# Where the rounded half of each weight piece is made: ScalarE's cast, or a converting DMA issued by GpSimd

## The chip, the cores and the metric

The kernel runs on one NeuronCore of one Trainium2 chip. The metric is the device time of one execution in microseconds (us), taken as the median over runs. The hardware profiler gives the start and length of every instruction of one execution, the DMA packets, and the clock that was granted to TensorE.

## The reference

Two layers over 512 tokens of width 1024, all in float32. Each layer is

```
xn = rmsnorm(x);  u, q, k, v, gA, gB = split(xn @ w_in)
h  = x + (sigmoid(gA) * pool(u) * scale + sigmoid(gB) * diffattn(q, k, v)) @ w_out
hn = rmsnorm(h);  gate, up = split(hn @ w_ffn_in)
x  = h + (silu(gate) * up) @ w_ffn_out
```

`diffattn` has four heads with two softmaxes each, q and k normed and partly rotated, with a mask by chunks of 64 tokens, and a norm behind it; `pool` is a difference of window means (windows of 2, 4, 8 and 16 tokens) times a 256x256 matrix per group. The hidden width of the feed-forward part (FFN) is 2816.

## The kernel before, in words

**Two halves.** TensorE's fast float32 format (float32r) keeps only some of the bits. So every operand is split into a rounded half `hi` and a rest `lo` = value - `hi`, and every product is three matmuls into one accumulator: hi*hi, hi*lo, lo*hi (`product`, lines 210 to 218; in the profile L215, L216 and L217). `split` (L166, L167) does it: ScalarE (ACT) copies the value into a float32r tile, which rounds, and VectorE (DVE) subtracts that from the value.

**Weight pieces.** All weight matrices are cut into 244 pieces of 256 rows by 512 columns (512 KB, a tile of 128 partitions by 1024 numbers), in the order of their use (`weight_plan`). `piece` (from line 175) fetches the next one: SyncE (SP) issues a DMA from HBM into a `raw` tile (L180, three buffers), ACT casts it to `whi` (L166, eight buffers), DVE subtracts into `wlo` (L167, eight buffers). The first four pieces load into other tiles, since nothing else lies there yet.

**Blocks.** A block of four (or three, or one) pieces serves one set of products over all 512 tokens: for each of four heads the columns of q and k, of v and gate B, of u and gate A; then the output projection, and the FFN in three rounds of hidden tiles. A block's pieces are all read by its last product, so the four `whi` buffers come free one behind the other at the block's end, and the pieces for the block after next take them.

**The order.** TensorE (PE) is kept busy by a list of postponed steps: a step that needs a result of other engines is put off until PE has streamed a given number of columns (`later`, `run_due`). On each engine, the order of instructions is fixed when the program is built, by a scheduler that follows the kernel's order and its own estimates; at run time each engine takes its instructions strictly in that order, and an instruction that has to wait holds up all behind it.

**Places that the prediction speaks of.** (1) The merge of a head's two branches (`merged`): the pool product `y`, then on DVE two instructions on `ta` (L493, L494), a split of the result by ACT (L172, tile `mh`) and DVE (L173, tile `ml`), each for two halves of 128 features. The output projection reads `mh` and `ml`. (2) q and k of a token tile: ACT sums squares (L418), DVE and GpSimd (POOL) make the reciprocal root `r` (L230 on DVE, L231 on POOL, a power), DVE scales into `qn` (L422) and rotates it (L286 to L291), and PE transposes it (L221). (3) The norm in front of a layer or of the FFN (`normed`): ACT's squares (L251), `r`, DVE's `xs` (L255), PE's transposes, the split into `xh`, `xl`. POOL does nothing in the kernel before but the 80 powers and some set-up.

Of the kernel before, what the change touches and what calls it, by code (L numbers as in the profile page):

```python
# [10 lines left out]
F32 = mybir.dt.float32  # L11
# [15 lines left out]
ROT = 32  # L27
# [3 lines left out]
EPS = 1e-6  # L31
WINDOWS = (2, 4, 8, 16)
MASKED = -3.0e38
# Hidden tiles of the FFN in three rounds.
ROUNDS = ((0, 8), (8, 16), (16, 22))
# Rows of `rows`, per layer: q gain, k gain, lambda vectors, sub-norm gain.
R_QG, R_LAM, R_SG = 0, 256, 768
ORDER = (3, 2, 1, 0)
# The hidden tiles lie where the attention's tiles lay: from which tile on, under which tag, how many.
HIDDEN_AT = {0: ("qk", 4), 4: ("v", 2), 6: ("u", 2), 8: ("m", 2), 10: ("qk", 4), 14: ("v", 2), 16: ("u", 2), 18: ("m", 2),  # L40
             20: ("qk", 4)}
# How many columns TensorE streams between a step and the one of its chain that follows on TensorE.
QK_WAIT, SCORE_WAIT, PROB_WAIT, AV_WAIT, NORM_WAIT, MERGE_WAIT = 20400, 33600, 25200, 11400, 15000, 15000


def weight_plan():
    """The weight pieces in the order of their use: (name, layer, first row tile, columns)."""
    plan = []

    def block(name, layer, cols, k0=0, k1=KD):  # L50
        for k in range(k0, k1, 2):
            plan.append((name, layer, k, cols))

    def span(*parts):
        return [c for a, n in parts for c in range(a, a + n)]

    def qk(j):
        return span((1024 + 256 * j, 256), (2048 + 256 * j, 256))

    def vg(j):  # L60
        return span((3072 + 256 * j, 256), (5120 + 256 * j, 256))

    def ug(j):
        return span((256 * j, 256), (4096 + 256 * j, 256))

    for layer in range(L):
        def out(heads):
            for cb in range(2):
                for j in heads:
                    block("w_out", layer, span((512 * cb, 512)), 2 * j, 2 * j + 2)  # L70

        for i, j in enumerate(ORDER):
            block("w_in", layer, qk(j))
            if i >= 2:
                out(ORDER[i - 2:i - 1])
            block("w_in", layer, vg(j))
            if i:
                block("w_in", layer, ug(ORDER[i - 1]))
        block("w_in", layer, ug(ORDER[3]))
        out(ORDER[2:])  # L80

        def ffn_in(f):
            block("w_ffn_in", layer, span((P * f, 256), (FF + P * f, 256)))

        def ffn_out(f0, f1):
            for cb in range(2):
                block("w_ffn_out", layer, span((512 * cb, 512)), f0, f1)

        for r, (f0, f1) in enumerate(ROUNDS):
            for f in range(f0, f1, 2):  # L90
                ffn_in(f)
                if r and f == f0:
                    ffn_out(*ROUNDS[r - 1])
        ffn_out(*ROUNDS[-1])
    return plan
# [3 lines left out]
def trunk_kernel(  # L99
# [11 lines left out]
    nc = tc.nc  # L111
# [34 lines left out]
        return row.partition_broadcast(P)  # L146

    def lambdas():
        """The negated weights of the second softmax."""
        for layer in range(L):  # L150
            lam_init = 0.8 - 0.6 * math.exp(-0.3 * layer)
            lv, nl = lams[layer], neglam[layer]
            lp = sb.tile([P, 2, QK], F32, name="lp", tag="qn", bufs=3)
            nc.vector.tensor_mul(lp, lv[:, :, 0, :], lv[:, :, 1, :])
            l2 = const.tile([P, 2], F32, name=f"l2{layer}")
            nc.vector.tensor_reduce(l2, lp, axis=AX.X, op=ALU.add)
            nc.scalar.activation(l2, l2, AF.Exp)
            nc.vector.tensor_sub(nl, l2[:, 1:2], l2[:, 0:1])
            nc.vector.tensor_scalar_add(nl, nl, -lam_init)
# [2 lines left out]
    at = [0]  # L162

    def split(hi, lo, src):
        """src = hi + lo exactly, each of 12 significant bits."""
        ins = nc.scalar.copy(hi, src)  # L166
        nc.vector.tensor_sub(lo, src, hi.bitcast(F32))  # L167
        return ins

    def split_half(hi, lo, src):  # L170
        """As split, of src / 2."""
        nc.scalar.activation(hi, src, AF.Copy, scale=0.5)  # L172
        nc.vector.scalar_tensor_tensor(lo, src, 0.5, hi.bitcast(F32), op0=ALU.mult, op1=ALU.subtract)  # L173

    def piece(raw=None):
        i = at[0]
        at[0] += 1
        if raw is None:
            raw = sb.tile([P, 2, 512], F32, name="raw", tag="raw", bufs=3)
        nc.sync.dma_start(raw.rearrange("p a b -> p (a b)"), wts[i])  # L180
        hi = sb.tile([P, 2, 512], F32R, name="whi", tag="whi", bufs=8)
        lo = sb.tile([P, 2, 512], F32R, name="wlo", tag="wlo", bufs=8)
        split(hi, lo, raw)
        return [(hi[:, a, :], lo[:, a, :]) for a in range(2)]

    def wblock(n):
        """n row tiles of 512 columns: (hi, lo) by row tile."""
        return [pair for _ in range(n // 2) for pair in piece()]

    # Work that waits for other engines: (due by TensorE's columns, order, what).  # L190
    clock = [0]
    waiting = []
    count = [0]
# [4 lines left out]
        count[0] += 1  # L198

    def run_due(done=None):  # L200
        """What is due by now, or everything in its order until done()."""
        if running[0]:
            return
        running[0] = True
        while waiting and (waiting[0][0] <= clock[0] if done is None else not done()):
            heapq.heappop(waiting)[2]()
        running[0] = False
        assert done is None or done()

    def product(acc, pairs):  # L210
        """acc = the sum over pairs of (lhsT hi, lo), (rhs hi, lo)."""
        n = len(pairs)
        for i, ((ah, al), (bh, bl)) in enumerate(pairs):
            run_due()
            nc.tensor.matmul(acc, lhsT=ah, rhs=bh, start=i == 0, stop=False)  # L215
            nc.tensor.matmul(acc, lhsT=ah, rhs=bl, start=False, stop=False)  # L216
            nc.tensor.matmul(acc, lhsT=al, rhs=bh, start=False, stop=i == n - 1)  # L217
            clock[0] += 3 * acc.shape[-1]
# [3 lines left out]
        clock[0] += 2 * P  # L222

    def rsqrt_mean(ss, n, width, times=(1.0,)):
        """times * (ss / n + eps) ** -0.5, the factors each for an equal part of the columns."""
        r = sb.tile([P, width], F32, name="r", tag="r", bufs=4)
        part = width // len(times)
        for i, f in enumerate(times):
            cs = slice(i * part, (i + 1) * part)
            nc.vector.tensor_scalar(r[:, cs], ss[:, cs], 1.0 / (n * f * f), EPS / (f * f), op0=ALU.mult, op1=ALU.add)  # L230
        nc.gpsimd.tensor_tensor(r, r, mhalf[:, :width], op=ALU.pow)  # L231
        return r
# [12 lines left out]
        return [g[:, h * 512:(h + 1) * 512] for h in range(2)]  # L245

    def normed(key, t, xh, xl, g):
        """Token tile t of the residual, over its root mean square and by the gain, transposed into xh + xl."""
        xs = sb.tile([P, D], F32, name="xs", tag="mj", bufs=2)
        ss = small("ss")  # L250
        nc.scalar.activation(xs, res[t], AF.Square, accum_out=ss)  # L251
# [27 lines left out]
        return [sb.tile([P, n, S], F32R, name=name + part, tag=tag, bufs=2) for part in "hl"]  # L279

    def rotate(qn, t):
        """The first ROT of each head's features, in place."""
        ca = cos_t[:, t, :].unsqueeze(1).broadcast_to([P, 4, ROT])
        m1 = sb.tile([P, 4, ROT], F32, name="m1", tag="m1", bufs=2)
        m2 = sb.tile([P, 4, ROT], F32, name="m2", tag="m2", bufs=2)
        nc.vector.tensor_mul(m1, qn[:, :, :ROT], ca)  # L286
        for a in range(2):
            sa = sin_t[:, t, a * HALF:(a + 1) * HALF].unsqueeze(1).broadcast_to([P, 4, HALF])
            b = (1 - a) * HALF
            nc.vector.tensor_mul(m2[:, :, a * HALF:(a + 1) * HALF], qn[:, :, b:b + HALF], sa)  # L290
        nc.vector.tensor_add(qn[:, :, :ROT], m1, m2)  # L291
# [14 lines left out]
    xh, xl = new_xT()  # L306
# [20 lines left out]
    for layer in range(L):  # L327
# [9 lines left out]
            return [(h[:, c0:c1], l[:, c0:c1]) for h, l in pairs]  # L337

        def attention(j, before, then):
            """The head's inputs; its output, (1 + tanh(gate / 2)) * the normed sum, transposed, follows token by token."""  # L340
            if before is not None:
                need(*((layer, before, "s", t) for t in range(NT)))
            qh, ql = pair("q", "qk", 4)
# [105 lines left out]
            return [(hi[:, a, :], lo[:, a, :]) for a in range(2)]  # L449

        def windowed(j, c, acc, uh, ul):
            """The window means less the tile's own values, by shifted sums."""
            window = WINDOWS[j]
            up = sb.tile([P, 16 + S], F32, name="up", tag="up", bufs=2)
            nc.vector.memset(up[:, :16], 0.0)
# [12 lines left out]
            split(uh[:, c, :], ul[:, c, :], prev[:, 16:])  # L468

        def merged(j, mj, mh, ml):  # L470
            """The pool branch and the sum of both branches, transposed."""
            w = wblock(KD)
            pw = pool_weights(j)
            uh, ul = pair("u", "u", 2)
# [121 lines left out]


def constants():
    """What depends on the shapes alone: rotary factors and pool counts, by token."""
    import numpy as np  # L600

    f = np.float32
# [48 lines left out]
```

## Time and profile before

| what | value |
|---|---|
| median of three runs | 1483.15 us (1483.08 to 1483.3) |
| profiled execution, first to last instruction | 1481.0 us |
| PE busy | 1473.8 us, 6998 matmuls |
| DVE busy | 793.8 us |
| ACT busy | 531.6 us |
| POOL busy | 62.3 us |
| DMA, mean rate | 93 GB/s |
| granted TensorE clock | 1.000 |

The span of the profiled execution is 2.15 us under the median of the runs; what lies around the span (start and end of the program) makes the difference. Busy time of PE is wall time in which a matmul is under way. Matmuls overlap in PE's pipeline, so the mean length of one (0.38 to 0.40 us) is longer than the distance of two that follow each other (about 0.23 us).

### The profile page before, as it was taken

The page shows a single profiled execution, that of the slowest core. Times are in us where ns is not written, and L with a number is a line of the kernel's source. Part 1 is how long each engine was busy: PE and PEld are TensorE (multiplying, and loading weights), DVE is VectorE, ACT ScalarE, POOL GpSimd, SP SyncE. Part 2 cuts the span into 40 slices and gives each one's busy share as a digit, 9 for nine tenths or more (in the row PEclk, how much of TensorE's full clock was granted, in tenths as well). Part 3 has the DMA queues.
Part 4 walks back from the last instruction along what each step waited for, and adds up shares of the span by engine and source line. Part 5 has one row for each costly group of instructions (what it writes and reads, how often), then busy time and mean ns, then how long its engine had stood idle before and what let it go on. Part 6 is the DMA issues. An engine that isn't in the chain of part 4 may idle for free.

```text
span 1481.0 us, 18060 instructions
## 1 busy us (share of the span) xinstructions
PE 1473.8 (100%) x6998; PEld 1227.6 (83%) x6998; DVE 793.8 (54%) x1550; ACT 531.6 (36%) x1081; POOL 62.3 (4%) x87
## 2 busy tenths in 40 slices
PE   8999999999999999999999999999999999999999
PEld 6888888888988888888888888888889888888887
DVE  7767676566634334433476676766655433434331
ACT  6545343453323222312354543435433322222220
POOL 1010000000000000000010001000000000000000
PEclk9999999999999999999999999999999999999999
DMA  6322231223233223313222232222313223323311
GB/s 245 115 65 79 78 108 59 91 95 98 86 99 114 99 72 114 114 58 113 100 86 71 73 106 65 85 85 86 114 57 115 96 75 114 99 72 114 111 47 57
DMA packets 39832, 138.19 MB, mean 93 GB/s; under 512 B 4545, under 2 KB 5441, under 8 KB 39746
## 3 DMA queue, kind: packets, MB, share of 16 engines
q1 hardware_dynamic: 38450, 134.41, 27.5%
q10 hardware_dynamic: 1296, 2.62, 0.6%
q8 instruction: 55, 0.90, 0.3%
q14 instruction: 31, 0.25, 0.0%
HBM read 134.92 MB, written 2.10 MB: 93 GB/s over the span
## 4 chain that ended last, share of the span: by engine, by line
PE 98%; DVE 1%; ACT 0%; DMA 0%; POOL 0%; issue 0%; POOLq 0%; DVEq 0%; ACTq 0%
PE mm L217 30%; PE mm L215 30%; PE mm L216 30%; PE tr L221 3%; PE sc L217 1%; PE sc L216 1%; PE sc L215 1%; PE oy L217 1%; PE oy L216 1%; PE oy L215 1%; DVE xs L255 0%; DVE wlo L167 0%; ACT xs L251 0%; DMA res<-in_x 0%; DVE res L503 0%; POOL r L231 0%
## 5 line engine op out<-in xcount | busy, mean ns | idle before, releaser
L215 PE MATMUL mm<-xh,whi 128*128 128x512 f32 (+1 forms) x960 | 369.1, 385 | 0.0
L217 PE MATMUL mm<-xh,wlo 128*128 128x512 f32 (+1 forms) x960 | 367.1, 382 | 0.0
L216 PE MATMUL mm<-xl,whi 128*128 128x512 f32 (+1 forms) x960 | 366.9, 382 | 0.0
L166 ACT CAST whi<-raw 128x1024 fp32r<-128x1024 f32 x244 | 255.5, 1050 | 294.0 <-PE mm L217 139.4
L167 DVE TENSOR_TENSOR wlo<-raw,whi 128x1024 fp32r<-128x1024 f32 x244 | 297.5, 1222 | 117.2 <-ACT whi L166 109.0
L217 PEld LDWEIGHTS mm<-xh,wlo 128*128 128x128 f32 x960 | 180.4, 188 | 35.1
L216 PEld LDWEIGHTS mm<-xl,whi 128*128 128x128 f32 x960 | 180.6, 188 | 34.2
L215 PEld LDWEIGHTS mm<-xh,whi 128*128 128x128 f32 x960 | 180.5, 188 | 34.1
L215 PE MATMUL mm<-whi,xh 128*128 128x512 f32 x512 | 205.8, 402 | 0.1
L217 PE MATMUL mm<-whi,xl 128*128 128x512 f32 x512 | 200.9, 392 | 0.0
L216 PE MATMUL mm<-wlo,xh 128*128 128x512 f32 x512 | 200.7, 392 | 0.2 <-DVE wlo L167 0.2
L215 PE MATMUL mm<-whi,fh 128*128 128x512 f32 (+1 forms) x358 | 140.2, 391 | 0.0
L217 PE MATMUL mm<-whi,fl 128*128 128x512 f32 (+1 forms) x358 | 139.7, 390 | 0.0
L216 PE MATMUL mm<-wlo,fh 128*128 128x512 f32 (+1 forms) x358 | 139.1, 389 | 0.0
L503 DVE TENSOR_TENSOR res<-mm,res 128x512 f32<-128x512 f32 (+1 forms) x97 | 66.1, 683 | 132.4 <-PE mm L217 132.1
L217 PEld LDWEIGHTS mm<-whi,xl 128*128 128x128 f32 x512 | 96.3, 188 | 20.9 <-DVE xl L167 0.2
L215 PEld LDWEIGHTS mm<-whi,xh 128*128 128x128 f32 x512 | 96.5, 188 | 18.6 <-ACT xh L166 0.6
L216 PEld LDWEIGHTS mm<-wlo,xh 128*128 128x128 f32 x512 | 96.7, 189 | 18.4 <-DVE wlo L167 0.6
L231 POOL TENSOR_TENSOR r<-r,mhalf 128x1 f32<-128x1 f32 (+1 forms) x80 | 61.6, 770 | 1054.8 <-DVE r L230 979.4
L544 DVE SCALAR_TENSOR_TENSOR th<-th,mm 128x512 f32<-128x512 f32 x42 | 28.9, 688 | 122.9 <-ACT th L543 122.8
L217 PEld LDWEIGHTS mm<-whi,fl 128*128 128x128 f32 x358 | 67.4, 188 | 15.4
L216 PEld LDWEIGHTS mm<-wlo,fh 128*128 128x128 f32 x358 | 67.5, 188 | 15.0
(113 smaller groups left out, 1548.9 us busy)
## 6 DMA issues: line engine op xcount, KB each, us to landing
raw<-in_wts SPq DMA_DIRECT2D x244, 512.0 KB, 4.0
pwr<-in_pool_w ACTq DMA_DIRECT2D x8, 256.0 KB, 2.6
out<-res SPq DMA_DIRECT2D x7, 256.0 KB, 2.0
res<-in_x SPq DMA_DIRECT2D x3, 512.0 KB, 8.3
g<-in_gains SPq DMA_DIRECT2D x3, 512.0 KB, 3.7
res<-in_x ACTq DMA_DIRECT2D x1, 512.0 KB, 3.5
lv<-in_rows SPq DMA_DIRECT2D x2, 256.0 KB, 5.3
qkg<-in_rows SPq DMA_DIRECT2D x2, 128.0 KB, 6.6
```

The lines of the kernel that those rows point to most:

```text
L166: ins = nc.scalar.copy(hi, src)
L167: nc.vector.tensor_sub(lo, src, hi.bitcast(F32))
L215: nc.tensor.matmul(acc, lhsT=ah, rhs=bh, start=i == 0, stop=False)
L216: nc.tensor.matmul(acc, lhsT=ah, rhs=bl, start=False, stop=False)
L217: nc.tensor.matmul(acc, lhsT=al, rhs=bh, start=False, stop=i == n - 1)
L221: nc.tensor.transpose(dst, src, ident)
L231: nc.gpsimd.tensor_tensor(r, r, mhalf[:, :width], op=ALU.pow)
L503: nc.vector.tensor_add(res[t][:, cs], here, res[t][:, cs])
L544: nc.vector.scalar_tensor_tensor(th, th, 1.0, gate, op0=ALU.add, op1=ALU.mult)
```

## The change

From the ninth piece on, ACT's cast goes. Instead POOL issues a second DMA for the same piece, from the same place in HBM into `whi`, whose type differs from the source's, so that the DMA converts. DVE's subtraction stays; it now waits for two DMAs. The first eight pieces are split as before. What else the file differs in is comments, which moves its line numbers by four behind `piece`.

```diff
         nc.sync.dma_start(raw.rearrange("p a b -> p (a b)"), wts[i])
         hi = sb.tile([P, 2, 512], F32R, name="whi", tag="whi", bufs=8)
         lo = sb.tile([P, 2, 512], F32R, name="wlo", tag="wlo", bufs=8)
-        split(hi, lo, raw)
+        if i < 8:
+            split(hi, lo, raw)
+        else:
+            nc.gpsimd.dma_start(hi.rearrange("p a b -> p (a b)"), wts[i])
+            nc.vector.tensor_sub(lo, raw, hi.bitcast(F32))
         return [(hi[:, a, :], lo[:, a, :]) for a in range(2)]
```

The order of instructions moves with it. On DVE, the first merge of layer 0 stood like this before (`wlo` is the subtraction for the pieces of a later block, `ta` and `ml` belong to the merge):

```order
L167 TENSOR_TENSOR wlo<-raw,whi 128x1024 x3
L493 SCALAR_TENSOR_TENSOR ta<-ta,mm 128x512
L167 TENSOR_TENSOR wlo<-raw,whi 128x1024
L494 SCALAR_TENSOR_TENSOR ta<-ta,scale,mj 128x512
L493 SCALAR_TENSOR_TENSOR ta<-ta,mm 128x512
L173 SCALAR_TENSOR_TENSOR ml<-ta,mh 128x512
L494 SCALAR_TENSOR_TENSOR ta<-ta,scale,mj 128x512
L173 SCALAR_TENSOR_TENSOR ml<-ta,mh 128x512
```

and now:

```order
L187 TENSOR_TENSOR wlo<-raw,whi 128x1024 x2
L497 SCALAR_TENSOR_TENSOR ta<-ta,mm 128x512
L187 TENSOR_TENSOR wlo<-raw,whi 128x1024
L498 SCALAR_TENSOR_TENSOR ta<-ta,scale,mj 128x512
L497 SCALAR_TENSOR_TENSOR ta<-ta,mm 128x512
L187 TENSOR_TENSOR wlo<-raw,whi 128x1024
L173 SCALAR_TENSOR_TENSOR ml<-ta,mh 128x512
L498 SCALAR_TENSOR_TENSOR ta<-ta,scale,mj 128x512
L173 SCALAR_TENSOR_TENSOR ml<-ta,mh 128x512
```

The same four subtractions and the same six steps of the merge stand there; the third and the fourth subtraction moved one and two places back, and all four still stand ahead of the first `ml`.

On POOL, at the third head of layer 0 (128x4 rows are the powers for q and k of one token tile, 128x1 rows those of the other norms), the powers stood alone before; the third head's four are the row before the last:

```order
L231 TENSOR_TENSOR r<-r,mhalf 128x1
L231 TENSOR_TENSOR r<-r,mhalf 128x4
L231 TENSOR_TENSOR r<-r,mhalf 128x1
L231 TENSOR_TENSOR r<-r,mhalf 128x4 x2
L231 TENSOR_TENSOR r<-r,mhalf 128x1 x4
L231 TENSOR_TENSOR r<-r,mhalf 128x4 x4
L231 TENSOR_TENSOR r<-r,mhalf 128x1 x4
```

Now DMAs stand among them; the third head's four powers are these rows' second, fourth and sixth:

```order
L186 DMA whi<-in_wts 128x1024 x4
L235 TENSOR_TENSOR r<-r,mhalf 128x4
L186 DMA whi<-in_wts 128x1024 x2
L235 TENSOR_TENSOR r<-r,mhalf 128x4 x2
L186 DMA whi<-in_wts 128x1024 x4
L235 TENSOR_TENSOR r<-r,mhalf 128x4
```

So the four DMAs of the q and k block stand behind the third token tile's power, and the fourth tile's power stands behind them.

On PE, at the last merge of layer 0, the output projection starts with products that read an earlier head's `mh_2967` and `ml_2968`, and then needs the last head's `mh_3244` and `ml_3245`. Before, behind its first six products, stood:

```order
L215 MATMUL mm_3456<-whi_3436,mh_3244 128x512
L216 MATMUL mm_3456<-wlo_3437,mh_3244 128x512
L215 MATMUL mm_3470<-whi_3442,mh_2967 128x512
L216 MATMUL mm_3470<-wlo_3443,mh_2967 128x512
L217 MATMUL mm_3470<-whi_3442,ml_2968 128x512
L215 MATMUL mm_3470<-whi_3442,mh_2967 128x512
L217 MATMUL mm_3456<-whi_3436,ml_3245 128x512
```

Now, behind its first eleven products:

```order
L219 MATMUL mm_3456<-whi_3436,mh_3244 128x512
L220 MATMUL mm_3456<-wlo_3437,mh_3244 128x512
L221 MATMUL mm_3470<-whi_3442,ml_2968 128x512
L219 MATMUL mm_3470<-whi_3448,mh_3244 128x512
L220 MATMUL mm_3470<-wlo_3449,mh_3244 128x512
L219 MATMUL mm_3492<-whi_3430,mh_2967 128x512
L220 MATMUL mm_3492<-wlo_3431,mh_2967 128x512
L221 MATMUL mm_3492<-whi_3430,ml_2968 128x512
L221 MATMUL mm_3456<-whi_3436,ml_3245 128x512
```

The first product that reads `ml_3245` was the 13th of the projection and is the 20th now, since products of other tiles were put ahead of it.

## The prediction

> **What bounds the kernel now.** I read the page first: span, busy time, clock, DMA, and the chain that ended last.
>
> ```profile
> span 1481.0 us, 18060 instructions
> ...
> PE 1473.8 (100%) x6998; PEld 1227.6 (83%) x6998; DVE 793.8 (54%) x1550; ACT 531.6 (36%) x1081; POOL 62.3 (4%) x87
> ...
> PEclk9999999999999999999999999999999999999999
> ...
> q1 hardware_dynamic: 38450, 134.41, 27.5%
> ...
> PE 98%; DVE 1%; ACT 0%; DMA 0%; POOL 0%; issue 0%; POOLq 0%; DVEq 0%; ACTq 0%
> ```
>
> TensorE is busy for all but 7.2 us, at the full granted clock, and it is 98% of the chain. The busy time by stretches (after the bounds and the length: PE, PEld, DVE, ACT, POOL) says where the 7.2 us lie:
>
> ```profile
> 0.00:20.00 20.00, 16.18 (x60) 10.93 (x61) 12.79 (x24) 13.41 (x26) 2.94 (x11) 1.00 0.91 335
> 20.00:1400.00 1380.00, 1379.93 (x6585) 1152.31 (x6584) 756.19 (x1496) 505.55 (x1039) 59.41 (x76) 1.00 0.28 91
> 1400.00:1481.00 81.00, 77.72 (x357) 64.36 (x355) 24.77 (x33) 12.61 (x17) 0.00 (x0) 1.00 0.20 72
> ```
>
> From 20 to 1400 us PE idles 0.07 us. The rest is the start, whose pieces the change leaves alone, and the end. So the change has nothing to win; the question is only whether something comes late at PE that came in time before.
>
> **What is removed and added.** By groups (count, busy us, mean ns), and the life of a `raw` tile:
>
> ```profile
> L167 DVE TENSOR_TENSOR wlo<-raw,whi 128x1024 fp32r<-128x1024 f32 x244 | 297.5, 1222 | 117.2 <-ACT whi L166 109.0
> L166 ACT CAST whi<-raw 128x1024 fp32r<-128x1024 f32 x244 | 255.5, 1050 | 294.0 <-PE mm L217 139.4 <-DMA raw<-in_wts 83.1 <-issue 34.9
> L231 POOL TENSOR_TENSOR r<-r,mhalf 128x4 f32<-128x4 f32 x32 | 33.2, 1038 | 236.5 <-DVE r L230 236.5
> ...
> L180 SPq DMA_DIRECT2D raw<-in_wts x244: 327/328/852, 1.1 to 1423.2; - x122
> ...
> DMA to landing us min/median/max: 3.3/4.0/7.6
> ```
>
> Removed: 236 casts of 1.05 us, 248 us of an engine that is busy 36%. Worth 0 by itself, as PE waits for ACT almost nowhere. Added: 236 DMAs of 512 KB. SP's queue moved 134.41 MB in 27.5% of the DMA engines' time; the new 124 MB bring it to about 53%, so in the mean there is room. DVE's 236 subtractions stay, 1.22 us each.
>
> What changes is the time X from a `whi` buffer's release by PE to its new content. It was about 1.1 us (release, then a cast). Now it is POOL's time to issue the DMA, and the DMA's way. The trace has no DMA of POOL. Bounds: an issue on SP takes 0.33 us, the dearest ordinary POOL instruction here 1.04; a landing comes 3.3 to 7.6 us after the issue, median 4.0. So X lies between 3.6 and 8.6. I take 1.04 + 4.0 = 5.0: POOL builds the descriptors itself, so I take its dearer row, and the median landing, since DMA traffic doubles. The page "DMA: Bandwidth & Descriptors" of the Trainium skill, section "Anatomy of one DMA — SWDGE (gpsimd) path", gives 2.0 us plus bytes over 436 GB/s for such a DMA, an estimate of 3.2 us here; by it X would be below everything that follows, and the time unchanged. No row here shows it.
>
> Does PE wait for `whi` itself? Its first reader is a block away:
>
> ```profile
> 166.38 1.05 ACT L166 CAST whi<-raw 128x1024 fp32r<-128x1024 f32 x1 [0.31 <-ACT qh L166]
> ...
> 188.19 0.39 PE L215 MATMUL mm<-whi,xh 128*128 128x512 f32 x1
> ```
>
> Ready at 167.4, read at 188.2: 20.8 us of cover against 4 us of lateness. The weights cost nothing. But the subtractions stand in DVE's fixed order, and DVE waiting for a landing holds up what stands behind. Four places have less cover than that.
>
> **Place A, the merge of the first and second head in each layer (4 times).** DVE, with ACT's first casts and PE's last need:
>
> ```profile
> 141.97 1.05 ACT L166 CAST whi<-raw 128x1024 fp32r<-128x1024 f32 x1 [0.55 <-PE mm L216]
> 143.33 1.05 ACT L166 CAST whi<-raw 128x1024 fp32r<-128x1024 f32 x1 [0.31 <-PE mm L216]
> ...
> 143.06 3.95 DVE L167 TENSOR_TENSOR wlo<-raw,whi 128x1024 fp32r<-128x1024 f32 x3 [1.49 <-ACT whi L166]
> 147.90 0.69 DVE L493 SCALAR_TENSOR_TENSOR ta<-ta,mm 128x512 f32<-128x512 f32 x1 [0.90 <-PE mm L217]
> 148.74 1.23 DVE L167 TENSOR_TENSOR wlo<-raw,whi 128x1024 fp32r<-128x1024 f32 x1 [0.16 <-ACT whi L166]
> 149.88 0.75 DVE L494 SCALAR_TENSOR_TENSOR ta<-ta,scale,mj 128x512 f32<-128x512 f32 x1
> 150.55 0.68 DVE L493 SCALAR_TENSOR_TENSOR ta<-ta,mm 128x512 f32<-128x512 f32 x1
> 151.33 0.69 DVE L173 SCALAR_TENSOR_TENSOR ml<-ta,mh 128x512 fp32r<-128x512 f32 x1
> 151.94 0.75 DVE L494 SCALAR_TENSOR_TENSOR ta<-ta,scale,mj 128x512 f32<-128x512 f32 x1
> 153.38 0.69 DVE L173 SCALAR_TENSOR_TENSOR ml<-ta,mh 128x512 fp32r<-128x512 f32 x1 [0.70 <-ACT mh L172]
> ...
> 155.70 0.39 PE L217 MATMUL mm<-whi,ml 128*128 128x512 f32 x1
> ```
>
> Buffers come free 1.36 us apart (141.97, 143.33), and instructions without a wait follow each other by 1.14 us behind a `wlo`, 0.61 to 0.67 behind a merge step. In the new order, from the first `wlo`'s start to the second `ml`'s end: 1.36 (second landing), 1.14, 0.61, 1.14, 0.67, 0.61, 1.14, 0.61, then 1.44 (ACT's `mh`, as between 151.94 and 153.38) and 0.69: 9.4 us. So `ml` ends at 141.97 + X + 9.4, and PE needs it at 155.70: X may be 4.3. At 5.0, PE waits 0.7 us; four times, **2.8 us**.
>
> **Place C, the last merge of a layer (twice).**
>
> ```profile
> 348.45 1.05 ACT L166 CAST whi<-raw 128x1024 fp32r<-128x1024 f32 x1 [0.47 <-PE mm L216]
> 359.36 0.69 DVE L173 SCALAR_TENSOR_TENSOR ml<-ta,mh 128x512 fp32r<-128x512 f32 x1 [0.70 <-ACT mh L172]
> 360.24 0.40 PE L217 MATMUL mm<-whi,ml 128*128 128x512 f32 x1
> ```
>
> Today `ml` ends 0.19 us before its reader. PE's new order puts seven more products ahead, 0.21 us each (1379.93 over 6585): 361.7. The same 9.4 us chain from 348.45 allows X = 3.9; at 5.0 PE waits 1.1, twice, **2.2 us**.
>
> **Place B, the fourth token tile of q and k, third and fourth head (4 times).**
>
> ```profile
> 178.72 1.01 POOL L231 TENSOR_TENSOR r<-r,mhalf 128x4 f32<-128x4 f32 x1 [4.43 <-DVE r L230]
> 184.37 0.67 DVE L167 TENSOR_TENSOR ql<-tr,qh 128x512 fp32r<-128x512 f32 x1
> 186.11 0.16 DVE L371 RECIPROCAL rc<-st 128x2 f32<-128x2 f32 x1
> ...
> 187.09 0.16 DVE L230 TENSOR_SCALAR r<-ss 128x2 f32<-128x2 f32 x1
> 188.44 1.13 DVE L422 SCALAR_TENSOR_TENSOR qn<-mm,r,qkg 128x128 f32<-128x128 f32 x4 [1.19 <-POOL r L231]
> 191.69 0.28 DVE L291 TENSOR_TENSOR qn<-m,m 128x128 f32<-128x128 f32 x1
> ...
> 193.11 0.27 PE L221 MATMUL tr<-ident,qn 128*128 128x128 f32 x1
> ```
>
> The four DMAs stand behind the power that ends at 179.73, so the first lands at 179.73 + X. On DVE follow two `wlo` (2.3), `ql` (0.6) and the six small ones (1.14), then POOL's power (1.19), then `qn`: at 184.95 + X, against 188.44 today. Its cover is 193.11 - 191.97 = 1.14, so X may be 4.6; at 5.0 the wait is 0.4, four times, **1.6 us**. The power is not late by the DMAs on POOL: the last buffer is free at about 182.7, five us ahead of it.
>
> **Place D, the second layer's first norm (once).**
>
> ```profile
> 744.84 2.13 ACT L166 CAST whi<-raw 128x1024 fp32r<-128x1024 f32 x2
> ...
> 752.69 0.69 DVE L167 TENSOR_TENSOR xl<-tr,xh 128x512 fp32r<-128x512 f32 x1
> 753.09 0.67 PE L221 MATMUL tr<-ident,xs 128*128 128x128 f32 x2
> ```
>
> PE's second transpose waits for this `xl`; there is no cover, and three `wlo` stand ahead on DVE. The lateness of X (up to 5.0 - 1.1 = 3.9 us) meets gaps in between; I take a third of it, **1.4 us**, between 0 and 3.9.
>
> In the FFN the DVE work behind the subtractions feeds accumulators that PE needs again two products later (24 matmuls of 0.21 us each: some 10 us), so X is hidden there: 0.
>
> **Sum** 2.8 + 2.2 + 1.6 + 1.4 = 8.0 us, on the profiled 1481.0: 1489.0. The runs' median lies 2.15 above the span: **1491**.
>
> **The rivals.** *Hidden anyway.* If X is 4.4 or less, A costs at most 0.4, C 1.0, D 0.8, B nothing: 2.2 us or less. For it: the shortest landing is 3.3 and the old DMAs leave the engines idle most of the time. Against: POOL's issue comes on top. 1484. The Trainium skill's page on DMA, cited above, would end here.
>
> *The conversion is slow.* If it halves a DMA engine's rate, 512 KB take 3.2 us of all engines instead of 1.6 (27.5% of 1481 are 407 us for 134.41 MB); four of those and four plain loads are 19 us of a block of 24 (1481 over 244, times four). The fourth landing comes 5.5 us later and X grows by 1.6, so A and C wait some 6 us each, B 3: 6 x 6 + 4 x 3 + 5 = 53, time 1536. Nothing in the trace speaks for or against.
>
> *POOL is held up by DVE.* If POOL cannot build descriptors while a DVE instruction runs, X grows by up to a `wlo`, 1.2 us, to 6.2: A 4 x 1.9, C 2 x 2.3, B 4 x 1.6, D 1.8: 20 us, 1504. The page "SBUF — State Buffer" of the Trainium skill, section "Who interferes with whom", states such a lock, but for DVE's two-port modes, and says a two-input subtraction blocks GpSimd's reads only. No trace with a DMA of POOL is here to agree or not.
>
> *Faster.* ACT free of 248 us delivers `mh` and `xh` earlier, and PE's waits shrink. They are 0.07 us between 20 and 1400 us; only the start could give, some 3.8 us, and it keeps ACT's casts. 1479.
>
> That the DMA does not round would change no duration here.
>
> **How the numbers follow.** X at 5.0 and around it (4.6 to 5.7, with some 10 us of waits per us of X: 1487 to 1498): 0.43. Hidden: 0.31. Slow conversion: 0.11. POOL held up: 0.11. Faster: 0.04. A change within 0.2% (3 us) can't be told from none. Faster 0.04, same 0.31, slower 0.65. The range leaves out the faster case below and, above, the slow conversion: 1482 to 1525.
>
> **What would show it.** In the profile after: DVE's `wlo` waits for the DMA of `whi`, some 4 us at the places A to D; PE waits for `ml`, `mh`, `qn` and `xl` there and nowhere for `whi`; ACT is busy about 285 us; the new queue moves 124 MB; a landing of POOL's DMAs near 5 us with its issue. It is wrong if PE's waits sit in the FFN, if the landing is under 4 us and PE still waits, or if DMA engines are busy far over half.

## The result, and the profile after

| | before | with the change |
|---|---|---|
| median of the runs, us | 1483.17 (1483.08 to 1483.3) | 1501.37 (1499.0 to 1502.84) |
| ratio, with its 95% interval | 1 | 1.0121 [1.0107, 1.0135] |
| profiled execution, us | 1483.15 | 1502.84 |
| its span, us | 1481.0 | 1501.1 |

The change costs 18.2 us, where 8 were forecast. First the page of the changed kernel: busy time, DMA queues (packets, MB, share), the chain that ended last, and the DMA issues (the last number is the median time from issue to landing).

```profile
PE 1482.1 (99%) x6998; PEld 1228.2 (82%) x6998; DVE 789.2 (53%) x1550; ACT 288.6 (19%) x845; POOL 188.4 (13%) x323
...
q0 software_dynamic: 33984, 123.75, 26.8%
q1 hardware_dynamic: 38450, 134.41, 26.7%
...
PE 71%; DMA 10%; DVE 9%; issue 7%; ACT 2%; POOL 2%; POOLq 0%; DVEq 0%; ACTq 0%
...
raw<-in_wts SPq DMA_DIRECT2D x244, 512.0 KB, 4.6
whi<-in_wts POOLq DMA_DIRECT2D x236, 512.0 KB, 4.7
```

ACT lost its 243 us and POOL gained 126. The converting DMAs move their 123.75 MB in 26.8% of the engines' time, almost the share of the plain ones for 134.41. TensorE's 98% of the chain became 71%. Next the waits of the changed kernel (who waited, for what: us in total, times, longest).

```profile
DVE wlo L187 <- DMA whi<-in_wts: 164.6, 88, 6.5
...
DVE wlo L187 <- DMA raw<-in_wts: 64.7, 41, 3.2
...
ACT pwh L166 <- DMA pwr<-in_pool_w: 35.6, 6, 8.1
...
PE mm L219 <- ACT mh L172: 5.0, 6, 1.0
PEld mm L221 <- DVE ml L173: 4.6, 9, 1.1
...
PE tr L225 <- DVE qn L295: 4.2, 4, 1.9
```

The first line is what the prediction counted on. The second and third are not in its sum: DVE also waits for the plain load, and ACT for the pool weights (`pwr` is the tile that they are loaded into, `pwh` their rounded half), for which it waited 0.7 us before. PE waits for `mh`, `ml` and `qn`, and nowhere for `whi`.

The table below gives TensorE's lost time by place. It is worked out from the starts of successive PE instructions in each timeline: what their distance exceeds the unstalled one (227 ns after a matmul of 512 columns, 120 after 256, 112 after 128), where that is over 80 ns. Time lost to a halved clock (last section) stands apart. "All" is the time from PE's first transposes to its last matmul, less that of before; the whole span exceeds that of before by 0.2 to 0.6 us more, and by 2.3 us more in the kernel with the pool weights in the ring of `ta`, which loses them at the very start. "All" is of one profiled execution, the last column is of medians. The kernels below the second are the experiments.

| kernel | A | B | C | D | clock | all | median over before |
|---|---|---|---|---|---|---|---|
| before | 0.6 | 0.7 | 0.0 | 0.5 | 0 | 0 | 0 |
| the change | 7.2 | 5.6 | 3.2 | 1.1 | 3.1 | 19.7 | 18.2 |
| FFN alone | 0.6 | 0.7 | 5.0 | 0.5 | 0 | 5.6 | 4.5 |
| attention alone | 8.3 | 4.2 | 0.0 | 1.3 | 0 | 12.8 | 15.7 |
| copy out | 0.9 | 0.7 | 1.6 | 0.8 | 0 | 2.7 | 2.3 |
| pool weights in ring of `ta` | 8.7 | 0.7 | 3.4 | 1.3 | 1.6 | 17.0 | 18.8 |
| merge first | 1.6 | 3.0 | 0.4 | 1.2 | 0 | 6.5 | 7.8 |
| `pwh` late | 7.4 | 0.7 | 3.4 | 1.3 | 1.6 | 13.9 | 15.6 |
| both orders | 1.5 | 0.7 | 0.4 | 1.3 | 0 | 4.7 | 5.2 |
| smaller rings | 7.6 | 3.9 | 3.9 | 1.3 | 1.6 | 18.7 | 20.0 |
| same, fourth `raw` | 4.7 | 0.7 | 3.1 | 1.3 | 0 | 8.3 | 11.1 |
| both orders, fourth `raw` | 1.5 | 0.7 | 0.4 | 1.4 | 0 | 4.5 | 3.7 |
| FFN alone, merge first | 0.6 | 0.7 | 0.4 | 0.6 | 0 | 0.6 | 0.5 |

The places are those that the prediction named. Now what happens at A. From the timeline of the changed kernel, POOL's issues, DVE's rows, SP's issues and PE's:

```profile
143.42 0.55 POOL L235 TENSOR_TENSOR r<-r,mhalf 128x1 f32<-128x1 f32 x1 [6.83 <-DVE r L234]
...
146.07 0.53 POOL L186 DMA_DIRECT2D whi<-in_wts  x1 [0.83 <-PE mm L220]
...
147.43 0.53 POOL L186 DMA_DIRECT2D whi<-in_wts  x1 [0.83 <-PE mm L221]
...
148.10 2.52 DVE L187 TENSOR_TENSOR wlo<-raw,whi 128x1024 fp32r<-128x1024 f32 x2 [3.15 <-DMA whi<-in_wts]
149.35 6.71 SPq L180 DMA_DIRECT2D raw<-in_wts  x4
...
154.48 1.23 DVE L187 TENSOR_TENSOR wlo<-raw,whi 128x1024 fp32r<-128x1024 f32 x1 [0.87 <-DMA raw<-in_wts]
155.54 0.40 PE L219 MATMUL mm<-whi,mh 128*128 128x512 f32 x1
...
157.66 0.69 DVE L173 SCALAR_TENSOR_TENSOR ml<-ta,mh 128x512 fp32r<-128x512 f32 x1 [0.69 <-ACT mh L172]
...
158.41 0.50 PE L221 MATMUL mm<-whi,ml 128*128 128x512 f32 x1
```

Buffers come free 1.36 us apart; the third at 146.07, so the first at 143.35. DVE starts its first `wlo` at 148.10: X is 4.75 us, against 5.0 forecast, though a power on POOL that ends at 143.97 holds the first issue up by 0.6. From there to the second `ml`'s end, at 158.35, it is 10.25 us and not 9.4: the fourth `wlo` waits 0.87 us for the plain load of its own `raw`. That load needs a `raw` tile, which the first of these very subtractions releases: SP issues it at 149.35, 6.0 us after the first `whi` buffer came free. Before, it was issued at 144.31, 2.3 us after. So two landings follow each other, the converting one and then the plain one.

At the second site of A and at C the first landing is sooner, and PE waits all the same. The second site of A (POOL, DVE), then C in the first layer (POOL, DVE, ACT, PE):

```profile
240.09 0.57 POOL L186 DMA_DIRECT2D whi<-in_wts  x1 [0.20 <-PE mm L221]
...
244.16 1.23 DVE L187 TENSOR_TENSOR wlo<-raw,whi 128x1024 fp32r<-128x1024 f32 x1 [3.29 <-DMA whi<-in_wts]
246.14 1.23 DVE L187 TENSOR_TENSOR wlo<-raw,whi 128x1024 fp32r<-128x1024 f32 x1 [0.76 <-DMA whi<-in_wts]
...
251.03 1.23 DVE L187 TENSOR_TENSOR wlo<-raw,whi 128x1024 fp32r<-128x1024 f32 x1 [0.67 <-DMA raw<-in_wts]
...
358.21 0.53 POOL L186 DMA_DIRECT2D whi<-in_wts  x1 [20.13 <-PE mm L221]
...
362.14 1.23 DVE L187 TENSOR_TENSOR wlo<-raw,whi 128x1024 fp32r<-128x1024 f32 x1 [7.11 <-PE mm L221]
363.91 1.23 DVE L187 TENSOR_TENSOR wlo<-raw,whi 128x1024 fp32r<-128x1024 f32 x1 [0.54 <-DMA whi<-in_wts]
...
367.66 0.63 ACT L172 ACTIVATE mh<-ta 128x512 fp32r<-128x512 f32 x1 [4.85 <-DVE ta L498]
...
368.34 0.50 PE L219 MATMUL mm<-whi,mh 128*128 128x512 f32 x1 [1.00 <-ACT mh L172]
```

POOL issues here as soon as PE releases the buffer, and X is 4.07 us (244.16 - 240.09) and 3.93 (362.14 - 358.21; that row puts its wait down to PE, but the DMA landed 3.9 us after its issue). The landings behind the first come later. Their buffers are free 1.36 us apart, but the second subtraction starts 1.98 and 1.77 us after the first, and the fourth piece lands 6.2 and 6.0 us after its issue. At C, PE waits for the first half's `mh`, not for the second `ml` that the prediction followed.

At B the row that matters is on ACT. From the timeline of the changed kernel, ACT's queue and ACT, then DVE, then PE:

```profile
189.54 0.34 ACTq L449 DMA_DIRECT2D pwr<-in_pool_w  x1
195.83 0.62 ACT L166 CAST pwh<-pwr 128x512 fp32r<-128x512 f32 x1 [8.06 <-DMA pwr<-in_pool_w]
196.35 0.58 ACT L166 CAST qh<-tr 128x512 fp32r<-128x512 f32 x1
...
196.96 0.69 DVE L167 TENSOR_TENSOR ql<-tr,qh 128x512 fp32r<-128x512 f32 x1 [2.85 <-ACT qh L166]
197.57 0.28 DVE L295 TENSOR_TENSOR qn<-m,m 128x128 f32<-128x128 f32 x1
...
198.00 0.94 PE L225 MATMUL tr<-ident,qn 128*128 128x128 f32 x4 [1.94 <-DVE qn L295]
```

The pool weights' tile `pwr` lives in the ring of `raw`. Its load is issued at 189.54, after DVE has released a tile of that ring, and lands 6.3 us later. ACT waits 8.06 us with the third tile's `qh` behind it, DVE waits for that `qh` with the fourth tile's `qn` behind it, and PE waits 1.94 us. Before, the load was issued at 184.5 and landed in 2.6.

### The profile page after: what moved, and what is told of

Read it like the earlier page. It is cut to its first block, busy times and chain, and to the rows that moved or that the text cites. A ratio compares the mean times of both kernels' runs of the same rounds, so it can differ in the third digit from the quotient of the medians.

```text
span 1501.1 us, 18222 instructions
## 1 busy us (share of the span) xinstructions
PE 1482.1 (99%) x6998; PEld 1228.2 (82%) x6998; DVE 789.2 (53%) x1550; ACT 288.6 (19%) x845; POOL 188.4 (13%) x323
## 3 DMA queue, kind: packets, MB, share of 16 engines
q0 software_dynamic: 33984, 123.75, 26.8%
q1 hardware_dynamic: 38450, 134.41, 26.7%
## 4 chain that ended last, share of the span: by engine, by line
PE 71%; DMA 10%; DVE 9%; issue 7%; ACT 2%; POOL 2%; POOLq 0%; DVEq 0%; ACTq 0%
PE mm L221 22%; PE mm L219 22%; PE mm L220 22%; DMA whi<-in_wts 5%; DMA raw<-in_wts 4%; DVE wlo L187 2%; PE tr L225 2%; DMA pwr<-in_pool_w 1%; DVE us L465 1%; POOL r L235 1%; PE sc L221 1%; PE sc L220 1%; PE sc L219 1%; DVE ul L167 1%; DVE al L167 1%
## 5 line engine op out<-in xcount | busy, mean ns | idle before, releaser
L187 DVE TENSOR_TENSOR wlo<-raw,whi 128x1024 fp32r<-128x1024 f32 x236 | 288.2, 1222 | 295.7 <-DMA whi<-in_wts 164.6
L186 POOL DMA_DIRECT2D whi<-in_wts x236 | 126.9, 538 | 842.2 <-PE mm L221 403.7
L220 PEld LDWEIGHTS mm<-wlo,xh 128*128 128x128 f32 x512 | 97.0, 189 | 18.8 <-DVE wlo L167 1.1
L219 PEld LDWEIGHTS mm<-whi,xh 128*128 128x128 f32 x512 | 96.9, 189 | 18.7 <-ACT xh L166 0.6
L547 ACT ACTIVATE th<-mm 128x512 f32<-128x512 f32 x42 | 25.1, 597 | 336.4 <-PE mm L221 336.4
```

The costliest lines, as they stand in the source:

```text
L186: nc.gpsimd.dma_start(hi.rearrange("p a b -> p (a b)"), wts[i])
L187: nc.vector.tensor_sub(lo, raw, hi.bitcast(F32))
L547: nc.scalar.activation(th, gate, AF.Tanh, scale=0.5)
```

## The experiments

Two theories were set against each other first. *Streams*: time is lost only where an instruction that PE needs soon stands behind a landing in the fixed order of DVE or ACT. *Traffic*: twice the DMA traffic makes everything late. (Further rivals stand with their runs.)

**Converting DMAs for the FFN's pieces alone.**

```diff
-        if i < 8:
+        if i < 8 or plan[i][0] in ("w_in", "w_out"):
```

> Converting DMAs for the 132 pieces of the FFN alone; the 104 later pieces of the attention are cast by ScalarE again. Theory S (streams): the loss arises only where an instruction that PE needs soon stands behind a wait for a landing in the fixed order of DVE or ACT, and all such places (the merges, the fourth token tile, the pool weights) lie in the attention. Then this kernel takes 1483 to 1485 us. Theory T (traffic): twice the DMA traffic makes landings late wherever it flows; then the FFN's 132 of 236 pieces bring 132/236 of the 18.2 us: 1493.

Measured: 1487.71 us, ratio 1.0029 [1.0018, 1.0039]. Neither number. The timeline of this kernel shows where (DVE and PE in the last merge of the first layer):

```profile
355.80 1.23 DVE L187 TENSOR_TENSOR wlo<-raw,whi 128x1024 fp32r<-128x1024 f32 x1 [0.60 <-DMA whi<-in_wts]
...
360.13 0.50 PE L219 MATMUL mm<-whi,mh 128*128 128x512 f32 x1 [1.03 <-ACT mh L172]
```

Nearly all of the loss is at C (5.0 of 5.6 us in the trace): the four pieces that stand between that merge's steps are the FFN's first. Place C was in the theory, but was counted to the attention. The test of this reading is the last run of the section.

**The attention's pieces alone.**

```diff
-        if i < 8:
+        if i < 8 or plan[i][0] not in ("w_in", "w_out"):
```

> The counterpart: converting DMAs for the 104 pieces of the attention, ScalarE's casts in the FFN. Theory S: all of the loss is here, 1499 to 1503 us. Theory T: 104/236 of 18.2 us, 1491.

Measured: 1498.86 us (1495.93 to 1502.2), ratio 1.0106 [1.0092, 1.012], just under the expected 1499. A and B are there, some 1 us up and down from the full change, and C is gone. Traffic by share would have been 1491.

**The traffic without anybody who waits for it.** The casts stay on ACT.

```diff
         split(hi, lo, raw)
+        if i >= 8:
+            nc.gpsimd.dma_start(spare[i], hi.rearrange("p a b -> p (a b)").bitcast(F32))
```

> The kernel before, with its casts on ScalarE, and beside it a DMA of GpSimd for each of the 236 pieces that copies the rounded part out to a scratch tensor in HBM, which nothing reads: the DMA engines' traffic and GpSimd's issues of the change, with nobody who waits for them. Theory S: a raw tile may land some 0.6 us later, as in the changed kernel (4.6 instead of 4.0), and that is covered: 1483 to 1486 us. Theory T: most of the loss returns, 1494 to 1501.

Measured: 1485.48 us, ratio 1.0016 [1.0007, 1.0024]. Its DMA issues:

```profile
raw<-in_wts SPq DMA_DIRECT2D x244, 512.0 KB, 5.4
spare<-whi POOLq DMA_DIRECT2D x236, 512.0 KB, 5.1
```

And one row of its waits, with ACT at C in the first layer:

```profile
ACT whi L167 <- DMA raw<-in_wts: 159.3, 59, 5.5
...
356.51 1.05 ACT L167 CAST whi<-raw 128x1024 fp32r<-128x1024 f32 x1 [2.47 <-DMA raw<-in_wts]
357.46 0.62 ACT L173 ACTIVATE mh<-ta 128x512 fp32r<-128x512 f32 x1
```

Plain loads land even later than in the changed kernel, 5.4 against 4.6, and ACT waits 159 us for them instead of 83. That costs 2.3 us, an eighth of the loss. So the traffic theory falls as the main cause, but its part is not zero. Most of that part comes through a stream again: 1.6 of the 2.7 us in its trace lie at C, where a cast on ACT waits 2.47 us for its plain load (1.10 before) with the `mh` that PE needs behind it.

**The pool weights in another ring.**

```diff
-            raw = sb.tile([P, 2, VD], F32, name="pwr", tag="raw", bufs=3)
+            raw = sb.tile([P, 2, VD], F32, name="pwr", tag="ta", bufs=2)
```

> The changed kernel, with the pool weights' raw tile in the ring of ta instead of the ring of raw, so that its load no longer waits until DVE has released a raw tile. Theory S with ACT's stream at place B: in the changed kernel ScalarE waits 7 to 8 us for this load at the fourth token tile, and the cast of qh behind it makes PE wait. The load then is issued 2 us earlier, B's stalls of 6.9 us (1.7 of them at the halved clock) shrink by 4 to 7: 1494.5 to 1497.5 us. Theory W: it is the landing of whi on DVE alone that makes B late, as the prediction had it, and ScalarE's wait is only beside it: 1500 to 1502.

Measured: 1501.96 us, ratio 1.0126 [1.0113, 1.014]: by its number, the rival. Its trace says otherwise. B is gone entirely (0.7, as before). But since nothing holds the first load back any more, the build put it at the very start, in front of the first norm. DVE and PE of this kernel, there:

```profile
7.99 0.69 DVE L167 TENSOR_TENSOR pwl<-pwr,pwh 128x512 fp32r<-128x512 f32 x1 [2.07 <-ACT pwh L166]
8.60 1.40 DVE L259 SCALAR_TENSOR_TENSOR xs<-res,r,sc 128x512 f32<-128x512 f32 x2
...
9.48 1.73 PE L225 MATMUL tr<-ident,xs 128*128 128x128 f32 x7 [3.46 <-DVE xs L259]
```

PE's first transposes start at 9.48 instead of 7.54 in the changed kernel: 1.9 us. A grew by 1.5. The run alone decides nothing, so B was tried again by order alone.

**Merge first.** The four subtractions that stood between a merge's steps are queued behind its last `ml`. The edit in words: line 499 keeps the instruction of the last `ml`, and the fifth to eighth piece traced after it take it:

```diff
-            nc.vector.tensor_sub(lo, raw, hi.bitcast(F32))
+            with (tc.issue_after(h.ins) if (h := held.pop() if held else None) else nullcontext()): nc.vector.tensor_sub(lo, raw, hi.bitcast(F32))
...
-                split_half(mh[:, c, :], ml[:, c, :], ta)
+                held[:] = [split_half(mh[:, c, :], ml[:, c, :], ta)] * 4 + [None] * 4
```

> The changed kernel, with the four subtractions that stand between the merge's steps on DVE (first, second and last merge of each layer) queued behind the merge's last step; no transfer is added or taken away. Theory S: the merge no longer waits for landings, and the stalls at A and C, 8.4 + 2.9 us in the trace of the change (1.7 of them at the halved clock), go: 1489 to 1492 us. Rival R: what makes the merge late is not the order but DVE's work or PE's new order; then the subtractions come later and the time stays at 1500 or rises.

Measured: 1490.92 us, ratio 1.0054 [1.0041, 1.0068]; 10.4 us less than the change. A falls from 7.2 to 1.6, C from 3.2 to 0.4, and B, with nothing done to it, from 5.6 to 3.0.

**`pwh` late.** ACT's cast of the pool weights is queued behind the fourth tile's `qh`; the load stays where it is.

```diff
-            split(hi, lo, raw)
+            with tc.issue_after(turned[0].ins): split(hi, lo, raw)
```

> The changed kernel, with ScalarE's cast of the pool weights queued behind the cast of the fourth token tile's qh; the load itself and the ring of raw are as they were. Theory S with ACT's stream at place B: ScalarE no longer holds the cast of the third tile's qh behind the landing of the pool weights, and the stalls of 6.9 us at the four places (1.7 of them at the halved clock) shrink to 0 to 2: 1494 to 1497 us. Theory W, the landing of whi on DVE alone: 1500 to 1502.

Measured: 1498.74 us, ratio 1.0108 [1.0095, 1.0122]; its runs lie between 1496.89 and 1502.51. The median misses the expected 1497 by 1.7 us, and its interval overlaps that of the change. B is what decides, and that is read from the trace: 5.6 to 0.7, while the order of DVE's `wlo` ahead of `qn` is what it was. ACT's stream is B's cause; the landing of `whi` on DVE, B's cause in the prediction, costs nothing there.

**Both orders.**

> Both edits of order together, on the changed kernel. Theory S: A, B and C go together, and with them the drops of the clock: 1483 to 1486 us, the time before, with all transfers of the change. If some of the loss has another cause (traffic, GpSimd's queue), 1487 to 1492.

Measured: 1488.31 us, ratio 1.0032 [1.0019, 1.0044]: 13.0 of the 18.2 us are back, not all. The waits of this kernel:

```profile
DVE wlo L187 <- DMA whi<-in_wts: 178.3, 86, 6.1
...
DVE wlo L187 <- DMA raw<-in_wts: 65.1, 41, 3.3
```

DVE waits for landings no less than in the changed kernel (164.6 and 64.7). It does so elsewhere, and there it is nearly free. The 5.2 us left were not taken apart. In the trace they are spread over stalls of at most 0.65 us behind the start. The 2.3 us of the copy out can't simply be taken off them, since most of those lay at C, which is at 0.4 here.

**A fourth `raw` tile, and its control.** SBUF has no 4 KB left, so four rings were made smaller in both.

```diff
-            raw = sb.tile([P, 2, 512], F32, name="raw", tag="raw", bufs=3)
+            raw = sb.tile([P, 2, 512], F32, name="raw", tag="raw", bufs=4)
```

> A control for the next kernel: the changed kernel with smaller rings that free 4 KB of SBUF (qn 3 to 2, mt 3 to 2, m1 and m2 2 to 1). If these rings do not bind, 1500 to 1503 us, as the changed kernel; if they do, some us more, and the next kernel is to be read against this one.

> The control, with a fourth raw tile in the space freed: the plain loads no longer wait for the subtraction that itself waits for a converting load. Theory S with the ring of raw: DVE's waits for raw landings (64.7 us in all in the changed kernel, 0.4 to 0.9 us of them inside each merge at A and C) nearly go; A and C win 0.4 to 0.9 us each at six places, 4 us, and B's pool weights are loaded earlier; the drops of the clock get rarer: 5 to 9 us below the control. Rival X: only the landing of whi counts; then 0 to 1 us.

Measured: the control 1503.14 us, ratio 1.0134 [1.012, 1.0149]; with the fourth tile 1494.28, ratio 1.0078 [1.0064, 1.0092]. 8.9 us less, as expected of the ring, and the runs of the two do not overlap (1500.03 to 1506.43 against 1491.55 to 1496.44). Waits of the kernel with four tiles:

```profile
DVE wlo L187 <- DMA whi<-in_wts: 218.2, 123, 6.2
...
ACT pwh L166 <- DMA pwr<-in_pool_w: 21.6, 6, 4.1
```

No row of DVE waiting for `raw` is left (70.0 us in the control). A falls by 2.9 and B to what it was before the change, as the pool weights' load is issued earlier (186.7 at the place shown above) and lands at 191.8. C falls by 0.8. The converting loads land as late as before, and A and C keep 4.7 and 3.1. The 1.6 us that the control loses to a halved clock are gone too.

**Both orders and the fourth tile.**

> Both edits of order and the fourth raw tile, on the smaller rings. Theory S: the small stalls left behind late raw landings (0.65 us at 76.6 us of the span with both edits) go as well: 2 us below the kernel with both edits, 1485 to 1487 us. If the copy out showed the floor that the traffic sets, it cannot be under 1485. Rival: 1488 or more, the rest has another cause or the smaller rings cost.

Measured: 1486.85 us, ratio 1.0026 [1.0016, 1.0037], 1.5 us under both orders alone and 3.7 over the kernel before.

**FFN alone, merge first.**

> Converting DMAs for the FFN's pieces alone, with the four subtractions at the last merge of a layer queued behind the merge's last step. The kernel with the FFN's pieces alone lost 4.5 us, and its trace shows 5.0 us of stalls at C, whose four pieces are the FFN's first. Theory S: they were all of it: 1483 to 1484.5 us. If the FFN itself loses by its traffic: 1486 to 1488.

Measured: 1483.66 us, ratio 1.0004 [0.9995, 1.0013], as before the change within the measurement. So the four subtractions at C were all that the FFN's converting DMAs cost. ACT is busy 395.7 us there instead of 531.6. That is the most that these runs got out of the change: no time, but room on ACT. Nothing beat the kernel before.

## Why the prediction was right or wrong

The direction held, and the measured time lies inside the range. The number was less than half of the loss: 8.0 us forecast, 18.2 measured.

**What bounds the kernel** held: nothing was won, and what was lost is PE's waiting. ACT is at 288.6 us, as said.

**X** was too high for the first landing, and one X does not fit all four. It is 4.75 and 4.70 us at the first and third site of A, where a power on POOL stands before the issue, 4.07 and 4.06 at the second and fourth, and 3.93 and 3.98 at C, against 5.0 taken. An issue takes POOL 0.53 us and not 1.04, and the time to landing counts from the start of the issue, so that the sum had the issue twice. The prediction allowed X 4.3 at A and 3.9 at C. By that, four of the six merges should have lost almost nothing, and their stalls are 1.6 to 2.3 us each. The row of the issues (duration in ns, min/median/max):

```profile
L186 POOL DMA_DIRECT2D whi<-in_wts x236: 527/527/714, 33.4 to 1461.6; - x118
```

**The failed step is "What changes is the time X from a `whi` buffer's release by PE to its new content".** X is not all that changes. The landings behind the first are later still, up to 6.2 us after their issue at the sites shown. And the subtraction that waits X also releases a `raw` tile, and that ring has three. So the plain loads start later by the same time, and the pool weights, which share the ring, too. The prediction treated `raw` as present. A fourth tile takes 8.9 us off against its control (in the profiled executions 2.9 at A, 3.2 at B, 0.8 at C, and 1.6 of halved clock). That is most of the size of what was missing, 10.2.

**Place A** (2.8 forecast, 6.6 over before in the trace). At the first site: X is 0.25 under, the wait for `raw` adds 0.87, and the cover is 0.4 smaller than the 13.73 us (155.70 - 141.97) counted. PE would have come to the second `ml` at 155.54 + 5 x 0.227 = 156.68, 13.33 us after the release. 0.7 - 0.25 + 0.87 + 0.4 is 1.7, and the site shows 1.9. At the second site X is 0.93 under, the second landing adds 0.62, the wait for `raw` 0.67 and the cover 0.4: 1.5, and the site shows 1.7. Without the wait for `raw`, A costs 4.1 over before: the mechanism was right and its size 1.3 short.

**Place C** (2.2 forecast, 3.2 measured) had the wait on DVE right, and the wrong step behind it. The prediction followed the second `ml` and allowed X 3.9, which X all but met. What PE waits for is the first half's `mh`: PE would have read it at 367.18 (0.227 after the product at 366.95), and it was ready at 368.29 (367.66 + 0.63). Only three of the four subtractions stand ahead of that `mh`, so the stall stays with four `raw` tiles, and it goes with the order. That forecast and measurement lie so near is luck.

**Place B** (1.6 forecast, 4.9 over before) had the place right and the cause wrong. The chain through DVE's two `wlo` costs nothing; the pool weights' cast on ACT, which the prediction did not look at, is all of it. The rule that every wait on an engine holds what is queued behind it was applied to DVE and not to ACT.

**Place D** (1.4 forecast, 0.6 measured) was sized too high.

**FFN 0** held: FFN alone with the merge first is at 1.0004.

**Not in the sum**: the traffic, 2.3 us in the copy out (1.6 of them at C, through ACT), and TensorE's clock, which halves after the worst stalls: 3.1 us in the profiled execution.

With the ring out of the way, the sum is met, but not by its parts. The kernel with four `raw` tiles loses 4.1 at A, 3.1 at C, 0.8 at D and 0 at B over before: 8.0 in its profiled execution. That its parts miss by 1.3, 0.9, -0.6 and -1.6 and still meet the forecast is luck. Its median is 11.1 over before.

**The rivals.** *Hidden anyway* fell by the time, though not by its own condition: X is under its 4.4 at four of the six merges, and they stall all the same. The estimate of 3.2 us by the Trainium skill's page "DMA: Bandwidth & Descriptors", section "Anatomy of one DMA — SWDGE (gpsimd) path", does not agree with the trace's median of 4.7. *Slow conversion* fell: 123.75 MB in 26.8% against 134.41 in 26.7% is 9% more time for a byte, not twice. *POOL held up by DVE* does not show: the issue's longest is 0.71 us and its median equals its minimum, with DVE busy 53% of the span. *Faster* fell.

## What to carry to other kernels

When a load takes the place of a compute step, follow every buffer that the waiting instruction releases, and not only the one that the load fills: a ring of three turned one late landing into two in a row. In a series of loads, look at the later landings too, and not only at the first. Follow the wait on each in-order engine that has one, and look at what PE needs next behind it. The remedy was order, not bandwidth: DVE waited as long as before, but 13 of 18 us came back when the waiting instructions stood behind the urgent ones.

## What the runs showed of the hardware

TensorE's granted clock fell to half for 3.41 us after a bad stall, though no gap there was longer than 2.1 us. Stretches of the changed kernel (bounds, length; PE, PEld, DVE, ACT, POOL with their counts; granted clock, DMA share, GB/s):

```profile
194.76:198.17 3.41, 1.47 (x9) 0.88 (x8) 1.21 (x3) 1.38 (x3) 0.00 (x0) 1.00 0.50 159
198.17:201.58 3.41, 3.41 (x11) 2.83 (x10) 2.73 (x5) 1.03 (x3) 0.00 (x0) 0.50 0.45 115
...
993.48:996.89 3.41, 1.95 (x7) 1.01 (x7) 2.36 (x7) 1.66 (x9) 0.02 (x1) 1.00 0.60 189
996.89:1000.30 3.41, 3.41 (x10) 2.64 (x9) 2.87 (x9) 0.00 (x0) 1.02 (x1) 0.50 0.00 1
```

And of the kernel with the pool weights in the ring of `ta`:

```profile
991.12:994.53 3.41, 1.56 (x6) 0.73 (x4) 2.49 (x3) 0.47 (x1) 0.00 (x0) 1.00 0.45 148
994.53:997.94 3.41, 3.19 (x8) 2.47 (x9) 2.42 (x8) 1.81 (x10) 1.04 (x1) 0.50 0.51 203
```

And of the control with the smaller rings, a stretch after which the clock stayed:

```profile
196.89:200.30 3.41, 1.97 (x11) 1.74 (x12) 2.99 (x6) 1.26 (x5) 0.00 (x0) 1.00 0.09 36
```

The two drops of the changed kernel start 798.72 us apart, 234 times 3.413: the stretches lie on a fixed grid. In the five drops inside the spans of four kernels PE was busy 1.47 to 1.95 us of the stretch ahead (43 to 57%); with 1.97 (58%), in the control with the smaller rings, the clock stayed. On each trace's own grid, from the start to 1400 us, no stretch of the thirteen traces with 1.97 or more is followed by a drop, and each with 1.95 or less is. Whether the busy share alone decides was not tested. So a stall can bring a drop or not, by where it lies on the grid. At the fourth site of A the changed kernel lost 1.9 us in two waits within one stretch, the one at 993.48, and the clock fell. The kernel with `pwh` late lost 2.1 us at the same site, over two stretches with 2.58 us busy in each, and it stayed. A drop costs about 1.7 us, half of 3.41. This fits the scatter of kernels with such stalls, up to 6.4 us from run to run, where the kernel before scatters by 0.7: in the control with the smaller rings the fastest run, 1500.03, has a mean granted clock of 1.000, the slowest, 1506.43, one of 0.998. That it is the only reason was not shown. The Trainium skill's page "TensorE: Matmul & The Clock Gate", section "What's actually happening", has the free-running window of 3413 ns, and the traces agree. Its section "Why this matters for your kernels" asks for no gap over some 3 us; here less was enough, and the traces decide.
